# Attention's loads issued by GpSimd, with bias rows for both heads of a pair in one load

## The chip, the core and the metric

The kernel runs on one core of one Trainium2 chip. A core has five instruction queues that each run their own instructions in program order and wait for each other through semaphores: TensorE (PE in the profile, with PEld for weight loads), VectorE (DVE), ScalarE (ACT), GpSimd (POOL) and SyncE (SP, here only an issuer of DMAs). The metric is the device time of one execution in microseconds, as the median over runs.

## The reference, cut to what matters

The program is one layer of a trunk with two groups of heads, in float32, on 1024 latent tokens (a grid of 16 rows and 64 columns) and 256 context tokens. What matters for the change is neighbourhood attention: each latent query sees 8 rows by 16 columns of its grid with a learned relative bias, and all 256 cached context keys, in one softmax.

```python
def _neighbourhood_attention(q, k, v, k_ctx, v_ctx, rpb):
    ...
    bias = rpb[:, dr[:, None, :, None], dc[None, :, None, :]].astype(jnp.float32)
    s_loc = jnp.einsum('bhrqd,bhrikd->bhrqik', qg, k_band).astype(jnp.float32) * scale
    s_loc = jnp.where(col_in[None, None, None, :, None, :], s_loc + bias[None], NEG)
    s_loc = s_loc.reshape(B, H, R, W, wr * W)
    s_ctx = jnp.einsum('bhrqd,bhkd->bhrqk', qg, k_ctx).astype(jnp.float32) * scale
    p = jax.nn.softmax(jnp.concatenate([s_loc, s_ctx], axis=-1), axis=-1).astype(v.dtype)
    ...
```

Beside it stands the Hyena group, a long convolution done by Fourier transforms; then follow the output projection and the feed-forward part:

```python
    a = attend(q, k, v).transpose(0, 2, 1, 3).reshape(B, L, ATTN_WIDTH)
    hyo = _hyena(hy, k_f, filt_bias)
    merged = jnp.concatenate([_rmsnorm(a, grp_norm_g[:ATTN_WIDTH]),
                              _rmsnorm(hyo, grp_norm_g[ATTN_WIDTH:])], axis=-1)
    x = x + g1 * (merged @ w_out)
```

## The kernel before

The kernel runs through stages: modulation and filter spectra, the input projection (24 chunks of 128 columns, each split into a high and a low part and multiplied in three passes by `mm3`, L115 to L118), the hyena chains, attention, output projection, and the feed-forward part. A tile framework orders the instructions of all stages with an estimate of its own and places them in each engine's queue; within a queue nothing overtakes.

The input projection writes q, k and v to DRAM (`qd`, `kd`, `vd`). Its last two chunks are `qkv(3, 2)`, the values of the last pair of heads, and `hy_chunk(2, 3)`; `cached(3)` then turns the last cached keys and stores them with `kt` (L735).

**The hyena chains** (`chain(j)`, j = 0 to 3 for four channel blocks of the latent tokens, 4 for the context) run with a high priority beside the projection and attention. A chain does for each of two orders o: forward products (L802), their twiddles (ACT L814 and L815 feed DVE L816), butterflies on DVE (L822 to L827), the product with a filter spectrum K for each half h (L836 loads K by SP, L840 to L843 multiply), butterflies back (L847 to L852), twiddles (L857 to L859), inverse products (L871), and gates (L876 to L878 for o = 0, L882 to L884 for o = 1). SP stores the result to `hyd` (L889, L892). K has one buffer for even and one for odd chains, so half 1's K can only be loaded once L841 of half 0 has read the buffer. The output projection's weights (L1148) take the chains' memory, and so come after the last store.

**Attention** (`attend(p_)`, four pairs of heads) loads q, k, v and the cached values of its pair by SP (L1003 to L1009), and then the bias tables `tb`. There are three tables for each head of the pair (first block of columns, inner ones, last block), each of 128 query rows by 736 numbers. `bias_load` fills one table with 16 loads of 16 partitions by 4 columns by 64 numbers from `rpw` in DRAM (L958). That makes 6 x 16 = 96 loads for a pair and 384 in all, each of 64 runs of 256 bytes, and SP issues them in the same queue as the chains' K and data. A pair then goes through four blocks of 16 columns: scores (L1020) in two halves, bias added and maximum taken on DVE (L1041), exponentials on ACT (L1054, L1055), turning by PE (`turn`, L1064), eviction from PSUM by `evict`, alternately on DVE (L968) and ACT (L970), the product with v (`av_mm`, L978), and the division by the sums (`recips`, L986 to L995; L1110). `context()` does the context tokens' attention (L1082 to L1091). The tiles `sel` and `jrev`, cut from the identity, serve the division and the later row scales.

Of the kernel before, what the change touches and what calls it, by code (L numbers as in the profile page):

```python
# [11 lines left out]
F32 = mybir.dt.float32  # L12
# [7 lines left out]
P = 128  # L20
# [3 lines left out]
LT = LL + LC  # L24
NH, DH = 8, 64
# [4 lines left out]
NEG = -1e30  # L30
# [44 lines left out]
HALF_ROWS = ((0, 11), (4, 12))  # L75
# [11 lines left out]
def _build(nc, tc, top, V, A, G, T, Q, I, O, dbg, upto):  # L87
# [37 lines left out]
    ident = cst.tile([P, P], F32, name="ident")  # L125
# [373 lines left out]
    qd = dr.tile([4, P, LT], F32, name="qd")  # L499
    with ies:  # L500
# [3 lines left out]
        for gi, (s, col, tl) in enumerate(groups):  # L504
            xs = []
            for i in tl:
                src, row, _ = tiles[i]
                x = wp.tile([P, D], F32, tag="wada", name="x", bufs=4) if gi in XW else \
# [21 lines left out]
            n = P * len(tl)  # L530
# [46 lines left out]
    kd = dr.tile([4, P, LT + 256], F32, name="kd")  # L577
# [345 lines left out]
    tp = pool(es, "att", reuse_waits="tile")  # L923
    asq = tp.tile([P, LT], F32, name="asq")


    sel = tp.tile([P, 4, P], F32, name="sel")
    for h in range(2):
        for i in range(4):
            V.tensor_copy(sel[:, i, h * DH:(h + 1) * DH], ident[:, 4 * h + i:4 * h + i + 1].to_broadcast([P, DH]))  # L930
    jrev = tp.tile([P, P], F32, name="jrev")
    V.tensor_copy(jrev, ident[:, ::-1])
    lrow = [tp.tile([P, P], F32, name=f"lrow{i}") for i in range(2)]
    for t in lrow:
        V.memset(t, 0.0)
# [8 lines left out]
    for r in Pring:  # L944
        for t in r:
            G.memset(t[:, 0, :, 11:16], 0.0)
            G.memset(t[:, 1, :, 0:4], 0.0)
    def bias_load(h, var):

        t = tbs[h % 2][var]  # L950
        for half in range(2):
            for rq in range(8):
                r = 8 * half + rq
                r0 = min(max(r - 4, 0), 8)
                nr = HALF_ROWS[half][1]
                a, d = r0 - HALF_ROWS[half][0], r0 - r + 7
                tv = t[rq * 16:(rq + 1) * 16, HOFF[half]:HOFF[half] + nr * 32].rearrange("q (u x) -> q u x", u=4)
                Q.dma_start(out=tv[:, :, a * 8:a * 8 + 64], in_=rpw[var, :, h, :, d * 8:d * 8 + 64])  # L958

    def stat(name, n=2):  # L960
        return tp.tile([P, n], F32, tag=name, name=name, bufs=4)
# [1 line left out]
    def evict(ps):  # L963

        t = tp.tile([P, 512], F32, tag="pt", name="pt", bufs=4)
        evict.i += 1
        if evict.i % 2:
            V.tensor_copy(t, ps)  # L968
        else:
            A.copy(t, ps)  # L970
        return t
# [27 lines left out]

    def attend(p_):  # L1000

        q = tp.tile([P, LT], F32, tag="q", name="q", bufs=2)
        Q.dma_start(out=q, in_=qd[p_])  # L1003
        k = tp.tile([P, LT + 256], F32, tag="k", name="k", bufs=2)
        Q.dma_start(out=k, in_=kd[p_])
        vs = tp.tile([P, 12, P], F32, tag="vs", name="vs", bufs=2)
        Q.dma_start(out=vs[:, 0:10], in_=vd[:, :, p_ * P:(p_ + 1) * P].rearrange("n p x -> p n x"))
        for h in range(2):
            Q.dma_start(out=vs[:, 10:12, h * DH:(h + 1) * DH],  # L1009
                        in_=I["cache_ctx_v"][0, 0, 2 * p_ + h].rearrange("(n p) d -> p n d", p=P))  # L1010
        for var in range(3):
            for h in range(2):
# [10 lines left out]
        def scores(cb, l, l2, j):  # L1023

            u0, u1 = BLK[cb]
            nu = u1 - u0
            a0 = 2 * cb - 1 + u0
            var = (0, 1, 1, 2)[cb]
            qc = [slice((2 * cb + half) * P, (2 * cb + half + 1) * P) for half in range(2)]
            m = [stat(f"m{h}") for h in range(2)]  # L1030
            loc = [[], []]
            for half in range(2):
                r0, nr = HALF_ROWS[half]
                n = nu * nr * 8
                sl = bk("S").rearrange("p (h x) -> p h x", h=2)
                smm([sl[:, h, :n] for h in range(2)], qc[half], lambda r: kg[r, a0:a0 + nu, r0 * 8:(r0 + nr) * 8])
                for h in range(2):
                    reg = Pring[h][cb][:, half, :, r0:r0 + nr].rearrange("p u r c -> p u (r c)")
                    loc[h].append(reg)
                    tv = tbs[h][var][:, HOFF[half]:HOFF[half] + nr * 32].rearrange("p (u x) -> p u x", u=4)  # L1040
                    V.tensor_tensor_reduce(out=reg, in0=sl[:, h, :n].rearrange("p (u x) -> p u x", u=nu),  # L1041
                                           in1=tv[:, u0:u1], op0=ALU.add, op1=ALU.max, scale=1.0, scalar=-3.0e38,
                                           accum_out=m[h][:, half:half + 1])
            sc = bk("S").rearrange("p (h x) -> p h x", h=2)
            for half in range(2):
                smm([sc[:, h, half * 256:(half + 1) * 256] for h in range(2)], qc[half], lambda r: k[r, LT:])
            m2 = stat("n", 4)
            V.tensor_reduce(m2, sc.rearrange("p h (a x) -> p (h a) x", a=2), axis=AX.X, op=ALU.max, negate=True)
            pc = tp.tile([P, 2, 2, 256], F32, tag="pc", name="pc", bufs=3)
            for h in range(2):  # L1050
                V.scalar_tensor_tensor(m[h], m[h], -1.0, m2[:, 2 * h:2 * h + 2], op0=ALU.mult, op1=ALU.min)
                for half in range(2):
                    c = 4 * h + 2 * j + half
                    A.activation(loc[h][half], loc[h][half], AF.Exp, bias=m[h][:, half:half + 1], accum_out=l[:, c:c + 1])  # L1054
                    A.activation(pc[:, h, half], sc[:, h, half * 256:(half + 1) * 256], AF.Exp,  # L1055
                                 bias=m[h][:, half:half + 1], accum_out=l2[:, c:c + 1])
            Pc[cb] = pc
# [38 lines left out]
        for b in range(2):  # L1096
# [12 lines left out]
            bs = recips(l, 8)  # L1109
            V.tensor_mul(dst[:, 2 * b:2 * b + 2], av.rearrange("p (b r c) -> p b r c", b=2, r=16),  # L1110
                         bs.rearrange("p (b r c) -> p b r c", b=2, r=16))
        if p_ < 3:
            context()
            sq = asq if p_ == 0 else tp.tile([P, LT], F32, tag="q", name="sq", bufs=2)
            A.activation(sq, at4[:, p_], AF.Square)
            if p_:
                V.tensor_add(asq, asq, sq)
# [41 lines left out]

    def token_scales():  # L1160

        sq = tp.tile([P, LT], F32, tag="q", name="sq", bufs=2)
# [601 lines left out]
```

## Time and profile before

| | us |
|---|---|
| median of three runs | 1954.95 |
| the runs | 1950.76, 1954.95, 1959.55 |
| the profiled execution | 1947.16 |
| its span, first to last instruction | 1945.3 |
| mean granted TensorE clock | 0.954 |

Over the whole span PE is busy for 1739.3 us (89%), PEld for 1458.2 (75%), DVE for 1372.1 (71%), ACT for 885.5 (46%) and POOL for 256.7 (13%). The span in 40 slices of 48.6 us, with a digit for the busy tenths of each, shows where PE is not full:

```profile
PE   6899989999993686687599699999999999999998
DVE  4667648746776775776455788898877777566787
POOL 2354556531320000000010000000000000000001
```

Slices 13 to 20 (counted from 1), from about 583 to 970 us, are attention and the rest of the hyena chains. POOL does nothing there. A row of a timeline gives start, duration, engine, line, what is written from what, and in brackets how long the engine had been idle and what ended it. SPq is SP's issuing of a DMA, not the transfer.

### The profile page before, as it was taken

The numbers are of one execution on the slowest core, as the hardware profiler recorded it, in microseconds if no ns is written. First come the engines' busy times: TensorE is split into PE (matmuls) and PEld (weight loads), VectorE is DVE, ScalarE is ACT, GpSimd is POOL, SyncE is SP. The second block draws the span as 40 slices with busy tenths as digits, with TensorE's granted clock in tenths as the row PEclk, the third lists the DMA queues.
The fourth block names the chain that finished last, engine by engine and source line by source line (L and its number), as shares of the span: only waits on it lengthen the run. The fifth ranks groups of instructions, "written<-read, shape, count | busy, mean of one in ns | idle before, by whom it ended". The sixth has DMA issues, their size and how long they took to land.

```text
span 1945.3 us, 27592 instructions
## 1 busy us (share of the span) xinstructions
PE 1739.3 (89%) x9999; PEld 1458.2 (75%) x9999; DVE 1372.1 (71%) x2183; ACT 885.5 (46%) x1827; POOL 256.7 (13%) x227
## 2 busy tenths in 40 slices
PE   6899989999993686687599699999999999999998
PEld 1688877888771354354478599999999999888786
DVE  4667648746776775776455788898877777566787
ACT  4655445434332463453265544444444444443352
POOL 2354556531320000000010000000000000000001
PEclk9999989999996898898799899999999999999999
DMA  7424444455344434301433155544322222753563
GB/s 260 133 75 126 129 126 121 138 189 174 122 128 128 106 65 116 76 12 54 162 127 113 44 161 171 170 157 165 127 71 71 71 70 63 264 202 113 190 210 134
DMA packets 238266, 249.79 MB, mean 128 GB/s; under 512 B 56610, under 2 KB 187795, under 8 KB 237873
## 3 DMA queue, kind: packets, MB, share of 16 engines
q1 hardware_dynamic: 236168, 247.09, 40.5%
q8 instruction: 79, 1.29, 0.3%
q10 hardware_dynamic: 1705, 0.82, 0.2%
q14 instruction: 58, 0.48, 0.1%
q0 software_dynamic: 256, 0.11, 0.0%
HBM read 176.75 MB, written 71.20 MB: 127 GB/s over the span
## 4 chain that ended last, share of the span: by engine, by line
PE 55%; DVE 15%; DMA 11%; ACT 5%; SPq 5%; issue 5%; POOL 3%; DVEq 0%; POOLq 0%; ACTq 0%
PE psd L118 6%; PE psd L116 6%; PE psd L117 6%; SPq L958 4%; PE psp L118 4%; PE psp L116 4%; PE psp L117 4%; PE psa L116 2%; PE psa L117 2%; PE psa L118 2%; DMA wt<-in_w_down_dram 2%; PE psav L978 2%; PE psc L116 2%; PE psc L117 2%; PE psc L118 2%
## 5 line engine op out<-in xcount | busy, mean ns | idle before, releaser
L116 PE MATMUL psp<-hh,wh 128*128 128x512 f32 (+1 forms) x552 | 201.0, 364 | 2.3 <-ACT wh L121 1.9
L118 PE MATMUL psp<-hh,wl 128*128 128x512 f32 (+1 forms) x552 | 198.9, 361 | 0.5 <-POOL wl L122 0.5
L117 PE MATMUL psp<-hl,wh 128*128 128x512 f32 (+1 forms) x552 | 198.2, 359 | 0.0
L117 PE MATMUL psa<-T,ws 128*128 128x256 f32 (+1 forms) x528 | 165.2, 313 | 2.8 <-DVE T L1206 2.8
L116 PE MATMUL psa<-T,ws 128*128 128x256 f32 (+1 forms) x528 | 165.6, 314 | 2.4 <-ACT rows L1479 2.4
L118 PE MATMUL psa<-T,ws 128*128 128x256 f32 (+1 forms) x528 | 164.6, 312 | 0.0
L116 PE MATMUL psd<-wd,gs 128*128 128x512 f32 x360 | 140.3, 391 | 3.1 <-ACT gs L121 3.1
L117 PE MATMUL psd<-wd,gs 128*128 128x512 f32 x360 | 140.7, 391 | 0.0
L118 PE MATMUL psd<-wd,gs 128*128 128x512 f32 x360 | 123.9, 392 | 1.6 <-DVE gs L122 1.6
L116 PEld LDWEIGHTS psp<-hh,wh 128*128 128x128 f32 x552 | 104.8, 190 | 23.1 <-issue 6.2
L118 PEld LDWEIGHTS psp<-hh,wl 128*128 128x128 f32 x552 | 104.9, 190 | 15.2 <-issue 0.8
L116 PE MATMUL psc<-T,ws 128*128 128x384 f32 (+1 forms) x352 | 110.0, 313 | 6.8 <-ACT ws L121 6.8
L117 PEld LDWEIGHTS psp<-hl,wh 128*128 128x128 f32 x552 | 104.9, 190 | 14.0 <-issue 0.4
L1679 POOL TENSOR_TENSOR rs<-rs,mhalf 128x1 f32<-128x1 f32 x10 | 7.7, 772 | 810.7 <-DVE rs L1678 810.7
L117 PE MATMUL psb<-T,ws 128*128 128x384 f32 (+1 forms) x352 | 110.3, 313 | 0.7 <-DVE T L1206 0.7
L118 PE MATMUL psb<-T,ws 128*128 128x384 f32 (+1 forms) x352 | 110.1, 313 | 0.0
L117 PE MATMUL psc<-T,ws 128*128 128x384 f32 (+1 forms) x352 | 110.1, 313 | 0.0
L116 PE MATMUL psb<-T,ws 128*128 128x384 f32 (+1 forms) x352 | 109.8, 312 | 0.3 <-ACT T L1205 0.3
L118 PE MATMUL psc<-T,ws 128*128 128x384 f32 (+1 forms) x352 | 109.8, 312 | 0.0
L116 PEld LDWEIGHTS psa<-T,ws 128*128 128x128 f32 x528 | 101.0, 191 | 3.5 <-ACT rows L1479 3.4
L117 PEld LDWEIGHTS psa<-T,ws 128*128 128x128 f32 x528 | 101.2, 192 | 3.1 <-DVE T L1206 3.1
L118 PEld LDWEIGHTS psa<-T,ws 128*128 128x128 f32 x528 | 100.8, 191 | 0.0
(389 smaller groups left out, 4646.9 us busy)
## 6 DMA issues: line engine op xcount, KB each, us to landing
wada<-in_w_ada_dram SPq DMA_DIRECT2D x48, 512.0 KB
wr<-in_w_up_dram SPq DMA_DIRECT2D x44, 512.0 KB
gr<-gdr SPq DMA_DIRECT2D x44, 320.0 KB
wr<-in_w_in_dram SPq DMA_DIRECT2D x23, 512.0 KB
wt<-in_w_down_dram SPq DMA_DIRECT2D x44, 256.0 KB
tdr<-wt SPq DMA_DIRECT2D x44, 256.0 KB
gdr<-cv SPq DMA_DIRECT2D x22, 512.0 KB
wr<-tdr SPq DMA_DIRECT2D x20, 512.0 KB
```

Of the source, the lines that this page charges most:

```text
L116: T.matmul(out, ah, bh, start=start, stop=False, skip_group_check=True)
L117: T.matmul(out, ah, bl, start=False, stop=False, skip_group_check=True)
L118: T.matmul(out, al, bh, start=False, stop=stop, skip_group_check=True)
L958: Q.dma_start(out=tv[:, :, a * 8:a * 8 + 64], in_=rpw[var, :, h, :, d * 8:d * 8 + 64])
L978: T.matmul(av[h * DH:(h + 1) * DH, c0:c0 + 256], vt[:, h * DH:(h + 1) * DH], p[:, h * 256:(h + 1) * 256], start=start, stop=False, tile_po ...
L1679: G.tensor_tensor(rs, rs, mhalf, op=ALU.pow)
```

## The change

All of attention's loads move from SP to GpSimd. The bias tables of the two heads of a pair become one tile of 1472 columns, so `bias_load` fills both heads with one load of 16 partitions by 8 by 64 numbers: 48 loads for a pair, 192 in all, of 128 runs each. With q, k, v and the cached values POOL issues 212 DMAs for attention. q and k of the first pair and the three tables are asked for ahead of the rest of the stage (`qkload(0)`, `bias_load(0, var)`), into buffers that are placed, by tiles named "none" that only hold room, where the last but one projection chunk worked. The buffers of q and k are named by the pair's parity instead of taken in turn. `evict` gives every third eviction to DVE, not every second. The copies that make `sel` and `jrev` go from DVE to ACT.

```diff
-    HOFF = (0, HALF_ROWS[0][1] * 32)
+    HOFF = (0, HALF_ROWS[0][1] * 64)
...
-    tbs = [[tp.tile([P, NROW * 32], F32, name=f"tb{h}{v}") for v in range(3)] for h in range(2)]
-    for t in tbs:
-        for v in t:
-            G.memset(v, NEG)
...
+    tbs = [None] + [tp.tile([P, NROW * 64], F32, name=f"tb{v}") for v in (1, 2)]
+    tp.tile([P, 2, 2, 256], F32, tag="pc", name="none", bufs=3)
...
+    for tag, n in (("q0", LT), ("k0", LT + 256), ("k1", LT + 256)):
+        tp.tile([P, n], F32, tag=tag, name="none", bufs=1)
+    tp.tile([P, 12, P], F32, tag="vs", name="none", bufs=2)
+    tbs[0] = tp.tile([P, NROW * 64], F32, name="tb0")
...
-                tv = t[rq * 16:(rq + 1) * 16, HOFF[half]:HOFF[half] + nr * 32].rearrange("q (u x) -> q u x", u=4)
-                Q.dma_start(out=tv[:, :, a * 8:a * 8 + 64], in_=rpw[var, :, h, :, d * 8:d * 8 + 64])
+                tv = tbs[var][rq * 16:(rq + 1) * 16, HOFF[half]:HOFF[half] + nr * 64].rearrange("q (u x) -> q u x", u=8)
+                G.dma_start(out=tv[:, :, a * 8:a * 8 + 64],
+                            in_=rpw[var, :, 2 * p_:2 * p_ + 2, :, d * 8:d * 8 + 64].rearrange("q h u x -> q (h u) x"))
+
+    def qkload(p_):
+        q = tp.tile([P, LT], F32, tag=f"q{p_ % 2}", name="q", bufs=1)
+        G.dma_start(out=q, in_=qd[p_])
+        k = tp.tile([P, LT + 256], F32, tag=f"k{p_ % 2}", name="k", bufs=1)
+        G.dma_start(out=k, in_=kd[p_])
+        return q, k
+
+    first = qkload(0)
+    for var in range(3):
+        G.memset(tbs[var], NEG)
+        bias_load(0, var)
...
+            A.copy(sel[:, i, h * DH:(h + 1) * DH], ident[:, 4 * h + i:4 * h + i + 1].to_broadcast([P, DH]))
...
-        if evict.i % 2:
+        if evict.i % 3 == 0:
             V.tensor_copy(t, ps)
...
-        q = tp.tile([P, LT], F32, tag="q", name="q", bufs=2)
-        Q.dma_start(out=q, in_=qd[p_])
-        k = tp.tile([P, LT + 256], F32, tag="k", name="k", bufs=2)
-        Q.dma_start(out=k, in_=kd[p_])
+        q, k = qkload(p_) if p_ else first
...
-        for var in range(3):
-            for h in range(2):
-                bias_load(2 * p_ + h, var)
+        if p_:
+            for var in range(3):
+                bias_load(p_, var)
```

The framework orders the instructions of the stage anew. Three places of the new order follow; a name's number is a buffer's, `s_` tiles are a chain's, and "x8" counts equal instructions in a row.

On PE, at the start of attention, the difference of the two orders is this:

```order
 L871 MATMUL pscA<-s_5679,idft 128x256 x8
 L802 MATMUL pscA<-s_5800,dftf 128x256 x2
-L1020 MATMUL psS<-k,q 128x264 x2
-L1020 MATMUL psS<-k,q 128x288 x2
+L1038 MATMUL psS<-k,q 128x264 x2
+L1038 MATMUL psS<-k,q 128x288 x2
 L802 MATMUL pscA<-s_5800,dftf 128x256 x2
```

Only the line numbers of the scores differ: chain 1's inverse products (L871) and chain 2's first forward ones (L802) stand ahead of the first scores in both. On SP, a little later, the loads of chain 2's K stood among bias loads (L958) and now stand alone:

```order
-L1007 DMA vs<-vd 128x10x128
-L1009 DMA vs<-in_cache_ctx_v_dram 128x2x64 x2
-L958 DMA tb_6407<-rpw 16x4x64 x16
-L958 DMA tb_6410<-rpw 16x4x64 x16
-L836 DMA K<-Kd 128x1024
-L958 DMA tb_6408<-rpw 16x4x64 x11
-L836 DMA K<-Kd 128x1024
-L958 DMA tb_6408<-rpw 16x4x64 x5
-L958 DMA tb_6411<-rpw 16x4x64
+L836 DMA K<-Kd 128x1024 x2
 L788 DMA s_5894<-lxd 128x1024
```

So nothing but the chains' own loads and stores is left in SP's queue there. On DVE, at the end of attention, the last product of attention (L1110) had only chain 4 behind it:

```order
L882 TENSOR_TENSOR s_6241<-tt,pscA 128x256
L883 TENSOR_TENSOR s_6241<-tt,pscA 128x256
L884 TENSOR_TENSOR s_6241<-s_6241,s_6239 128x2x256
L1110 TENSOR_TENSOR at_6387<-psav,bs 128x2x16x16
L840 TENSOR_TENSOR s_6286<-s_6266,K 128x1024
L841 TENSOR_TENSOR s_6283<-s_6266,K 128x1024
```

Now it is L1128, and the second half of chain 3 follows it as well:

```order
L840 TENSOR_TENSOR s_6196<-s_6187,K 128x1024
L841 TENSOR_TENSOR s_6147<-s_6187,K 128x1024
L1128 TENSOR_TENSOR at_6387<-psav,bs 128x2x16x16
L842 TENSOR_TENSOR s_6147<-s_6147,s_6196 128x512
L843 TENSOR_TENSOR s_6147<-s_6147,s_6196 128x512
L840 TENSOR_TENSOR s_6203<-s_6187,K 128x1024
L841 TENSOR_TENSOR s_6147<-s_6187,K 128x1024
L842 TENSOR_TENSOR s_6147<-s_6147,s_6203 128x512
```

Here s_6147 belongs to chain 3's second order and s_6283 to chain 4. On POOL, the first pair's q, k and first table come first, then its values, then the second pair's q, k and values, and only then the first pair's other two tables; that second q waits, among others, for the store of `kt` (L735) by `cached(3)`. 21 of the 212 loads stand ahead of it.

More of the change, by code (lines that the diff above doesn't have):

```diff
@@ L924, in _build, with bias_load @@
     asq = tp.tile([P, LT], F32, name="asq")
-    sel = tp.tile([P, 4, P], F32, name="sel")
-    for h in range(2):
[L929 to L935, printed above, removed]
-    tbs = [[tp.tile([P, NROW * 32], F32, name=f"tb{h}{v}") for v in range(3)] for h in range(2)]
-    for t in tbs:
-        for v in t:
-            G.memset(v, NEG)
     BLK = ((1, 4), (0, 4), (0, 4), (0, 3))
     Pring = [[tp.tile([P, 2, b - a, 16, 8], F32, name=f"Pl{h}{i}") for i, (a, b) in enumerate(BLK)] for h in range(2)]
[L944 to L950, printed above, removed]
+    tbs = [None] + [tp.tile([P, NROW * 64], F32, name=f"tb{v}") for v in (1, 2)]
+    tp.tile([P, 2, 2, 256], F32, tag="pc", name="none", bufs=3)
+    tp.tile([P, 512], F32, tag="pt", name="none", bufs=4)
+    tp.tile([P, LT], F32, tag="q1", name="none", bufs=1)
+    for name, n in (("l", 8), ("l2", 8), ("m0", 2), ("m1", 2), ("n", 4), ("lc", 4)):
+        tp.tile([P, n], F32, tag=name, name="none", bufs=4)
+    tp.tile([P, 512], F32, tag="bs", name="none", bufs=2)
+    for tag, n in (("q0", LT), ("k0", LT + 256), ("k1", LT + 256)):
+        tp.tile([P, n], F32, tag=tag, name="none", bufs=1)
+    tp.tile([P, 12, P], F32, tag="vs", name="none", bufs=2)
+    tbs[0] = tp.tile([P, NROW * 64], F32, name="tb0")
+    def bias_load(p_, var):
         for half in range(2):
@@ L956, in bias_load @@
                 a, d = r0 - HALF_ROWS[half][0], r0 - r + 7
-                tv = t[rq * 16:(rq + 1) * 16, HOFF[half]:HOFF[half] + nr * 32].rearrange("q (u x) -> q u x", u=4)
-                Q.dma_start(out=tv[:, :, a * 8:a * 8 + 64], in_=rpw[var, :, h, :, d * 8:d * 8 + 64])
+                tv = tbs[var][rq * 16:(rq + 1) * 16, HOFF[half]:HOFF[half] + nr * 64].rearrange("q (u x) -> q u x", u=8)
[11 more added lines that the diff above has]
+        bias_load(0, var)
+        if var == 0:
+            for r in Pring:
+                for t in r:
+                    G.memset(t[:, 0, :, 11:16], 0.0)
+                    G.memset(t[:, 1, :, 0:4], 0.0)
+    sel = tp.tile([P, 4, P], F32, name="sel")
+    for h in range(2):
+        for i in range(4):
+            A.copy(sel[:, i, h * DH:(h + 1) * DH], ident[:, 4 * h + i:4 * h + i + 1].to_broadcast([P, DH]))
+    jrev = tp.tile([P, P], F32, name="jrev")
+    A.copy(jrev, ident[:, ::-1])
+    lrow = [tp.tile([P, P], F32, name=f"lrow{i}") for i in range(2)]
+    for t in lrow:
+        V.memset(t, 0.0)
     def stat(name, n=2):
@@ L1000, in attend @@
     def attend(p_):
[L1002 to L1005 removed]
+        q, k = qkload(p_) if p_ else first
         vs = tp.tile([P, 12, P], F32, tag="vs", name="vs", bufs=2)
[L1007 removed]
+        G.dma_start(out=vs[:, 0:10], in_=vd[:, :, p_ * P:(p_ + 1) * P].rearrange("n p x -> p n x"))
         for h in range(2):
[L1009 removed]
+            G.dma_start(out=vs[:, 10:12, h * DH:(h + 1) * DH],
                         in_=I["cache_ctx_v"][0, 0, 2 * p_ + h].rearrange("(n p) d -> p n d", p=P))
[L1011 to L1013 removed]
+        if p_:
+            for var in range(3):
+                bias_load(p_, var)
         kg = k[:, 0:LL].rearrange("p (u x) -> p u x", u=8)
```

6 lines of the change are left out of this document (3 added, 3 removed).

## Prediction

> **What bounds the kernel now.** I read the busy time of each engine in stretches first, to see where the code that changes runs. The columns are the stretch, its length, then busy time (and instructions) of PE, PEld, DVE, ACT and POOL, the granted clock, the DMA share and GB/s.
>
> ```profile
> 577.00:624.00 47.00, 12.76 (x44) 8.79 (x44) 29.98 (x55) 10.11 (x30) 0.00 (x0) 0.67 0.42 113
> 624.00:904.00 280.00, 213.20 (x1284) 125.22 (x1284) 195.52 (x426) 143.91 (x472) 0.00 (x0) 0.91 0.29 73
> 904.00:949.00 45.00, 19.57 (x63) 12.00 (x61) 21.79 (x31) 6.38 (x11) 0.00 (x0) 0.83 0.23 77
> ```
>
> Attention's matmuls run from 624 to 904 us, and PE is idle in 67 of these 280 us. Ahead of it lie 47 us with PE nearly empty, behind it 45 us in which only the last hyena chain runs. No engine is full, so the waits decide. PE's and DVE's timelines (start, duration, what, and in brackets the idle time before and what ended it) have these large ones:
>
> ```profile
> 613.94 1.19 PE L871 MATMUL pscA<-s,idft 128*128 128x256 f32 x2 [29.11 <-DVE s L859]
> 624.12 1.20 PE L1020 MATMUL psS<-k,q 64*128 64x264 f32 x8
> 671.09 1.12 PE L978 MATMUL psav<-pt,vs 128*64 128x256 f32 x4 [12.24 <-DVE pt L968]
> 745.01 1.12 PE L978 MATMUL psav<-pt,vs 128*64 128x256 f32 x4 [9.24 <-DVE pt L968]
> 818.31 1.12 PE L978 MATMUL psav<-pt,vs 128*64 128x256 f32 x4 [9.20 <-DVE at L1110]
> ...
> 604.78 1.23 DVE L840 TENSOR_TENSOR s<-s,K 128x1024 f32<-128x1024 f32 x1 [7.08 <-DMA K<-Kd]
> 624.99 0.43 DVE L1041 CUSTOM_DVE_ANT_0 Pl<-psS,tb 128x264 f32<-128x264 f32 x1 [1.32 <-DMA tb<-rpw]
> 666.80 1.23 DVE L840 TENSOR_TENSOR s<-s,K 128x1024 f32<-128x1024 f32 x1 [10.65 <-DMA K<-Kd]
> 741.99 1.23 DVE L840 TENSOR_TENSOR s<-s,K 128x1024 f32<-128x1024 f32 x1 [9.21 <-DMA K<-Kd]
> 815.29 1.23 DVE L840 TENSOR_TENSOR s<-s,K 128x1024 f32<-128x1024 f32 x1 [9.03 <-DMA K<-Kd]
> ```
>
> Read the two lists together. Each of PE's three long waits for an eviction or a product of DVE ends just after DVE's wait for a filter spectrum K (L840), which stands ahead of that eviction in DVE's order. So K is what is late. SP's rows, and the source line of the bias loads (count, shortest, median and longest duration in ns), say why:
>
> ```profile
> L958 SPq DMA_DIRECT2D tb<-rpw x384: 302/424/1779, 587.3 to 822.9; - x192
> ...
> 651.24 1.22 DVE L841 TENSOR_TENSOR s<-s,K 128x1024 f32<-128x1024 f32 x1
> 645.83 17.05 SPq L958 DMA_DIRECT2D tb<-rpw  x32
> 662.97 0.37 SPq L836 DMA_DIRECT2D K<-Kd  x1
> ...
> 662.97 3.80 DMA K<-Kd
> 930.69 3.63 DMA K<-Kc
> ```
>
> K has one buffer per chain parity. It was free when L841 ended at 652.5, but SP stood in a run of 32 bias loads, one per 0.53 us, and issued K only at 662.97. The transfer then took 3.80 us, little more than the 3.63 us late in the stage with no bias load about. The bound of the stage is thus SP's issuing order, through K, DVE and PE.
>
> **The change, part by part.**
>
> *Loads leave SP.* All 384 bias loads go, and 192 of twice the rows are issued by POOL. At 666.80 K could have been asked for at 652.5 and have landed at 656.3; DVE reached its turn at 656.1 (666.80 less 10.65), so the wait shrinks to about 0.2 us. The other two are alike, and in the new order eight to ten instructions of DVE (L842 and L843 among them) stand between the two L840 of such a pair, in which K can land. I book PE's waits, 12.24 + 9.24 + 9.20 = **30.7 us**; bounds 20 (a third falls back to other waits) and 33 (PE also loses its low-clock start, some 0.7 us each time).
>
> *The first pair's early loads.* q, k and the first bias table can be in SBUF before 600 us instead of 624. But PE's order has the same eight inverse products of a chain (L871) and two forward ones ahead of the first scores as before, and PE's 29.11 us wait is for DVE in that chain, not for attention's loads. So only the table's own lateness goes, the 1.32 us at 624.99, and the share of SP in the K wait at 604.78:
>
> ```profile
> 595.16 1.22 DVE L841 TENSOR_TENSOR s<-s,K 128x1024 f32<-128x1024 f32 x1
> ...
> 622.97 0.69 DVE L884 TENSOR_TENSOR s<-s,s 128x512 f32<-128x512 f32 x1
> ```
>
> L841 ended at 596.4; K from SP then lands at 600.2 in place of 604.78. That is 4.3 us, with the table 5.6; bounds 4 and 6. The early loads alone are worth little.
>
> *The end of attention.* In the new DVE order chain 3 is further behind when attention ends: its last product (L1128) stands right behind the first L841 of the chain's second half, while before only chain 4 was left. What follows is priced from rows of the same work standing alone:
>
> ```profile
> 623.09 1.10 PE L802 MATMUL pscA<-s,dftf 128*128 128x256 f32 x4 [1.43 <-DVE s L883]
> ...
> 903.38 1.11 PE L802 MATMUL pscA<-s,dftf 128*128 128x256 f32 x4
> 903.39 0.69 DVE L1110 TENSOR_TENSOR at<-psav,bs 128x512 f32<-128x512 f32 x1 [1.20 <-ACT bs L995]
> 907.48 1.22 DVE L840 TENSOR_TENSOR s<-s,K 128x1024 f32<-128x1024 f32 x1 [3.40 <-ACT s L805]
> ...
> 945.79 2.78 DMA hyd<-s
> ```
>
> From the end of L841: 3.8 us for K; 18.3 us from L840 to the next chain's first forward product (604.78 to 623.09); 4.1 us from that product to chain 4's L840 (903.38 to 907.48); 38.3 us to its store (907.48 to 945.79). Together 64.5 us, where before 42.4 us lie between L1110's start and the store. That is **22.1 us lost**; bounds 16 and 26. The output projection's weights wait for this store, so it is on the path in full.
>
> *What leaves attention in exchange.* That half of chain 3 no longer takes turns with the last blocks:
>
> ```profile
> 872.54 1.91 PE L978 MATMUL psav<-pt,vs 128*64 128x256 f32 x8 [1.66 <-DVE pt L968]
> 884.70 0.65 PE L1064 MATMUL psX<-ident,Pl 128*128 128x128 f32 x4 [2.71 <-DVE pt L968]
> 889.44 0.74 PE L871 MATMUL pscA<-s,idft 128*128 128x256 f32 x2
> 893.53 1.46 PE L871 MATMUL pscA<-s,idft 128*128 128x256 f32 x6
> 898.33 1.89 PE L871 MATMUL pscA<-s,idft 128*128 128x256 f32 x8
> ```
>
> 1.66 + 2.71 us of waits behind its DVE work and 4.1 us of its products: **8.5 us gained**; bounds 0 (other waits take their place) and 12.
>
> *Evictions and setup.* A third instead of half of the 96 evictions goes to DVE. The columns of the groups are busy us, mean ns, idle before.
>
> ```profile
> L968 DVE COPY pt<-psX 128x512 f32<-128x512 f32 x48 | 32.9, 685 | 12.0 <-PE psX L1064 12.0
> L842 DVE TENSOR_TENSOR s<-s,s 128x512 f32<-128x512 f32 x14 | 9.6, 684 | 0.2
> L1054 ACT ACTIVATE Pl<-Pl,m 128x264 f32<-128x264 f32 (+1 forms) x64 | 35.7, 558 | 26.5 <-DVE m L1051 26.3
> L1055 ACT ACTIVATE pc<-psS,m 128x256 f32<-128x256 f32 x64 | 29.7, 466 | 0.0
> L970 ACT COPY pt<-psX 128x512 f32<-128x512 f32 x48 | 28.2, 588 | 62.8 <-PE psX L1064 62.7
> ```
>
> Sixteen move: 11.0 us off DVE, 9.4 us onto ACT, whose evictions waited 62.7 us for PE and so have room. I take zero; bounds -9.4 and +11. The copies that make sel go to ACT in the same stretch and cancel alike.
>
> *POOL as issuer.* POOL is idle here (0.00 above). Its DMAs at the kernel's start and the transfer that holds up its queue:
>
> ```profile
> 2.04 0.58 POOL L295 DMA_DIRECT2D w<-in_filt_w_dram  x1
> 4.97 0.56 POOL L309 DMA_DIRECT2D GE<-in_t_z_dram  x1
> ...
> 582.71 1.72 DMA kd<-kt
> ...
> 872.92 0.45 DVE L1041 CUSTOM_DVE_ANT_0 Pl<-psS,tb 128x288 f32<-128x288 f32 x1
> ```
>
> A load of 64 rows held POOL 0.58 us, one of 17 rows 0.56. A bias load has 128 runs, which the trace does not show: bounds 0.56 and 1.16 (twice 64 rows). I take 0.6, as row count hardly told. The second pair's q waits until kd<-kt has landed at 584.4, and 191 of POOL's 212 loads stand from there on. The last table is wanted 31 us before attention's end (872.9 against 904.1), which I expect at 858.6 (945.8 - 22.7 - 64.5). With 2 us to land, loads cost nothing up to (858.6 - 31 - 586.4) / 191 = 1.26 us each. Both bounds lie below, so the term is zero.
>
> **Sum.** 30.7 + 5.6 - 22.1 + 8.5 = 22.7 us gained. The profiled execution took 1947.16 us (span 1945.3), so it would take 1924.5. It lies 7.8 us below the median of the three runs, 1954.95; on that median the forecast is **1932 us**. All bounds together give -11 and +46.
>
> **The rivals.**
>
> *POOL becomes the bound (slower).* Place: the last pair's tables, behind all other loads. From 1.38 us a load the gain is gone, from 1.43 the kernel is slower by over 0.5%. That takes descriptors which POOL cannot write while DVE works: 0.56 us plus a whole L841 of 1.22 is 1.78. At 1.6, the store comes at 586.4 + 306 + 31 + 64.5 = 988, 42 later: 1997 us. Against: both rows of POOL's DMAs show under 0.6 us. For: the 192 loads stand beside dense DVE work, and those rows, at the kernel's start, do not. The Trainium skill (SBUF — State Buffer, Who interferes with whom) has GpSimd's descriptor writing shut out only while DVE is in a two-port mode, as in copies within SBUF, and not by a tensor_tensor. Here the evictions read PSUM at 685 ns, as slow as L842's 684 for the same size, so by that rule the price stays at zero. Chance 0.09.
>
> *K is late for the transfers' sake, not SP's.* If the bias rows crowd the DMA engines, the 30.7 and 4.3 us stay and the sum is -12: 1967 us. The rows above speak against it: 3.80 beside 3.63 us. The Trainium skill (DMA: Bandwidth & Descriptors, Issuing engines are not separate DMA queues) says this: DMAs share 16 engines whoever starts them, and another issuer saves only sequencer time, usually small beside the transfer. The trace disagrees on small: 10.5 us of issuing against 3.80. Chance 0.04.
>
> *Evictions late on ACT (no change).* A score block puts eight exponentials on ACT, 4 x (0.558 + 0.466) = 4.1 us. If in each of 16 blocks one more eviction waits a quarter of that behind them, 16 us go, and 6 remain: 1949. For: two evictions in a row are now ACT's. Against: its 62.7 us of waiting. Chance 0.16.
>
> *The early loads let scores start early.* If PE fell to scores at 588, some 32 us more: 1900. PE's order speaks against it. Chance 0.07.
>
> **How the numbers follow.** The forecast has 0.64. Faster by over 0.5% (9.8 us, about what a measurement can tell from no change): 0.64 + 0.07 = 0.71; within it 0.16; slower 0.09 + 0.04 = 0.13. The range, 1909 to 1960, is the sum with its bounds (46 gained, 5 lost), takes in the no-change rival, and leaves out the two slower rivals and the early start: 0.20.
>
> **What would show it.** L840's waits for K between 640 and 820 gone, with K issued within 1 us of the L841 that frees it; first scores near 620, not near 590; the end of attention near 859 and the store about 64 us behind it; POOL's bias loads near 0.6 us each. Wrong would be: K waits of 9 us again, POOL without a pause to the last table, or a store as far behind attention's end as before.

## The result, and the profile after

The changed kernel took 1921.29 us (median of four runs, 1920.5 to 1925.38) beside 1954.28 us (1950.76 to 1959.55) for the kernel before: ratio 0.9833, with a 95% interval of 0.9806 to 0.986. That is 27 to 38 us faster. The forecast was 1932. The profiled execution took 1925.38 us, and the working gave 1924.5 from the profiled execution before; the two profiled executions lie on different sides of their medians, 7.1 us below the one and 4.1 above the other.

The stretches of the span of the changed kernel (columns as in the prediction) are cut at the first scores, the end of the last division by sums, and the last store of `hyd`; the first row is the kernel before between its first scores and its last division.

```profile
624.12:904.09 279.97, 213.17 (x1284) 125.30 (x1284) 195.60 (x426) 143.91 (x472) 0.00 (x0) 0.91 0.29 73
```

```profile
623.42:847.91 224.49, 197.87 (x1265) 116.63 (x1264) 169.97 (x387) 146.41 (x474) 82.22 (x154) 0.99 0.28 72
847.91:920.21 72.30, 37.65 (x80) 22.46 (x80) 36.85 (x52) 11.49 (x25) 0.00 (x0) 0.57 0.19 58
```

Attention is 55.5 us shorter, and PE's idle time in it fell from 66.8 to 26.6 us. But what follows attention grew from 42.4 to 73.0 us, counted from the start of the last division, and PE's clock there is 0.57. The waits that the prediction spoke of stand in DVE's and SP's timelines now as follows.

```profile
604.15 1.23 DVE L840 TENSOR_TENSOR s<-s,K 128x1024 f32<-128x1024 f32 x1 [3.35 <-DMA K<-Kd]
652.45 1.22 DVE L840 TENSOR_TENSOR s<-s,K 128x1024 f32<-128x1024 f32 x1
720.05 1.23 DVE L840 TENSOR_TENSOR s<-s,K 128x1024 f32<-128x1024 f32 x1 [1.08 <-DMA K<-Kd]
787.14 1.22 DVE L840 TENSOR_TENSOR s<-s,K 128x1024 f32<-128x1024 f32 x1
847.21 0.68 DVE L1128 TENSOR_TENSOR at<-psav,bs 128x512 f32<-128x512 f32 x1
851.17 1.23 DVE L840 TENSOR_TENSOR s<-s,K 128x1024 f32<-128x1024 f32 x1 [2.08 <-DMA K<-Kd]
...
920.21 0.37 SPq L892 DMA_DIRECT2D hyd<-s  x1
```

```profile
623.42 1.20 PE L1038 MATMUL psS<-k,q 64*128 64x264 f32 x8
860.23 1.22 PE L871 MATMUL pscA<-s,idft 128*128 128x256 f32 x2 [12.51 <-DVE s L859]
```

The three waits of 9 to 11 us for K are gone, and first scores come 0.7 us earlier. From the first scores to the last store, PE's only wait above 3 us now lies behind attention, for chain 3. POOL's bias loads, by their source line (count, shortest, median and longest duration in ns), took 531 ns each and hardly scattered:

```profile
L951 POOL DMA_DIRECT2D tb<-rpw x192: 528/531/573, 572.3 to 778.7; - x192
```

### The profile page after: what moved, and what is told of

It is laid out like the page before. It is cut to its first block, busy times and chain, and to the rows that moved or that the text cites. A ratio compares the mean times of both kernels' runs of the same rounds, so it can differ in the third digit from the quotient of the medians.

```text
span 1923.4 us, 27377 instructions
## 1 busy us (share of the span) xinstructions
PE 1742.3 (91%) x9999; PEld 1460.2 (76%) x9999; DVE 1358.3 (71%) x2158; ACT 893.5 (46%) x1852; POOL 371.1 (19%) x436
## 4 chain that ended last, share of the span: by engine, by line
PE 35%; DVE 14%; DMA 8%; issue 4%; ACT 4%; POOL 2%; SPq 0%; DVEq 0%; POOLq 0%; ACTq 0%
PE psd L118 5%; PE psd L116 5%; PE psd L117 5%; DMA wt<-in_w_down_dram 2%; PE psa L116 2%; PE psa L117 2%; PE psa L118 2%; DMA tdr<-wt 2%; POOL tb L951 2%; PE psc L117 1%; PE psc L118 1%; PE psc L116 1%; PE pscA L871 1%; PE psb L117 1%; PE psb L118 1%
## 5 line engine op out<-in xcount | busy, mean ns | idle before, releaser
L951 POOL DMA_DIRECT2D tb<-rpw x192 | 100.4, 531 | 35.7 <-DVE m L1059 20.3
L871 PE MATMUL pscA<-s,idft 128*128 128x256 f32 x160 | 55.1, 487 | 56.0 <-DVE s L859 45.1
L116 PEld LDWEIGHTS psa<-T,ws 128*128 128x128 f32 x528 | 101.4, 192 | 4.7 <-ACT rows L1497 4.7
```

The lines of the kernel that those rows point to most:

```text
L116: T.matmul(out, ah, bh, start=start, stop=False, skip_group_check=True)
L871: T.matmul(pa[:, i * 256:(i + 1) * 256], idft[:, i, h], Ys[:, h, i, xs], start=h == 0, stop=h == 1, skip_group_check=True)
L951: G.dma_start(out=tv[:, :, a * 8:a * 8 + 64], in_=rpw[var, :, 2 * p_:2 * p_ + 2, :, d * 8:d * 8 + 64].rearrange("q h u x -> q (h u) x"))
```

## The experiments

All numbers of the traces are in one table: "first scores" is the start of the first matmul of the scores, "attention" the time from there to the start of the last division, "tail" from that to the last store of `hyd`, and "both done" the time at which attention and the chains are finished. In two kernels the chains finish first.

| kernel | ratio to before, interval | first scores | attention | tail | both done |
|---|---|---|---|---|---|
| before | 1 | 624.1 | 279.3 | 42.4 | 945.8 |
| changed | 0.9833 [0.9806, 0.986] | 623.4 | 223.8 | 73.0 | 920.2 |
| after_again (the same) | 0.985 [0.9822, 0.9878] | 622.1 | 222.5 | 72.2 | 916.8 |
| sp_loads | 0.9858 [0.9823, 0.9892] | 624.6 | 225.3 | 67.2 | 917.1 |
| merge_only | 0.9843 [0.9812, 0.9874] | 623.2 | 249.8 | 45.7 | 918.7 |
| k_by_pool | 1.0006 [0.9991, 1.0022] | 620.3 | 261.8 | 69.6 | 951.6 |
| half_evict | 0.9894 [0.9857, 0.993] | 618.8 | 234.1 | 65.7 | 918.6 |
| late_loads | 0.9921 [0.9895, 0.9948] | 626.7 | 231.1 | 70.4 | 928.2 |
| split_loads | 1.0229 [1.0202, 1.0256] | 623.8 | 368.9 | - | 992.7 |
| warm_tail | 0.9873 [0.9844, 0.9901] | 621.7 | 222.8 | 72.1 | 916.6 |
| context_first | 0.9877 [0.9846, 0.9908] | 621.4 | 236.8 | 59.5 | 917.6 |
| context_hole | 0.9806 [0.9778, 0.9833] | 657.8 | 222.1 | 26.8 | 906.7 |
| merge_hole | 0.9824 [0.9804, 0.9845] | 659.3 | 245.1 | 3.7 | 908.1 |
| two_in_hole | 0.9974 [0.9958, 0.999] | 734.5 | 215.0 | - | 949.5 |

The yardstick, the changed kernel once more beside three of the others:

> The changed kernel itself, beside the next three on one chip, as their yardstick: ratio 0.981 to 0.986; attention 224 us long, hyd's last store 73 us behind its last division.

It came out as expected, and shows how far one profile can be trusted: both done 3.4 us earlier than in the first profile, and 3.8 us less behind that, where the instructions are the same.

### Who issues, or how many: sp_loads and merge_only

sp_loads lets SP issue all of attention's loads in the changed kernel; of the five lines that this changes, the one of the bias loads is shown:

```diff
-                G.dma_start(out=tv[:, :, a * 8:a * 8 + 64],
+                Q.dma_start(out=tv[:, :, a * 8:a * 8 + 64],
```

> The changed kernel with attention's loads issued by SP again, still 192 merged bias loads. If K is late because it stands behind bias loads in SP's queue (theory), DVE waits for K again between 600 and 850 us, by at least 5 us in two or three places (SP needs about 0.45 us for each of some 8 to 16 loads ahead of a K), attention lasts 235 to 260 us from its first scores to its last division (224 in the changed kernel, 279 in the kernel before), and the time lies 0.5 to 1.5% above the changed kernel's (ratio 0.988 to 1.000). If halving the count of loads was what helped, the waits stay below 2 us each and the ratio is that of the changed kernel, 0.983.

The stated theory held at the first of its places and fell at the others. DVE's wait for K near 600 us is back, ahead of the first scores:

```profile
603.91 1.23 DVE L840 TENSOR_TENSOR s<-s,K 128x1024 f32<-128x1024 f32 x1 [6.67 <-DMA K<-Kd]
```

But the waits that follow, between 640 and 850 us, are 1.31 us at most with all 192 loads in SP's own queue, attention lasts 225.3 us, and the ratio is within the intervals of the changed kernel. So the sharper cut: merge_only is the kernel before with merged loads and nothing else. It keeps the old order on PE, ACT and DVE, but for one reciprocal that comes two instructions later on DVE.

```diff
-    tbs = [[tp.tile([P, NROW * 32], F32, name=f"tb{h}{v}") for v in range(3)] for h in range(2)]
+    tbs = [tp.tile([P, NROW * 64], F32, name=f"tb{v}") for v in range(3)]
...
-                Q.dma_start(out=tv[:, :, a * 8:a * 8 + 64], in_=rpw[var, :, h, :, d * 8:d * 8 + 64])
+                Q.dma_start(out=tv[:, :, a * 8:a * 8 + 64],
+                            in_=rpw[var, :, 2 * p_:2 * p_ + 2, :, d * 8:d * 8 + 64].rearrange("q h u x -> q (h u) x"))
...
-            for h in range(2):
-                bias_load(2 * p_ + h, var)
+            bias_load(p_, var)
```

> The kernel before with one edit: the bias rows of both heads come in one load, 192 loads on SP in place of 384. PE, ACT and DVE keep the order of the kernel before instruction for instruction. Theory (what counts is the number of loads that stand in the queue, since SP takes about 0.43 us to issue one, of 64 runs or of 128): the waits for K between 600 and 820 us fall to 2 us or less each, attention shrinks from 279 us to 236 to 250 (30.7 us of PE's waits, and up to 8 us of its higher clock), the tail stays at 42 us, and the ratio is 0.978 to 0.986. Rival (the loads have to leave SP): two or more waits for K of 5 us or more stay, attention lasts over 262 us and the ratio is above 0.990.

In merge_only's trace: the stretch of attention; SP's bias loads by their source line; SP's and DVE's rows at the first K wait and at the place where the kernel before lost most.

```profile
623.15:873.68 250.53, 211.27 (x1284) 124.72 (x1284) 195.22 (x426) 144.19 (x472) 0.00 (x0) 0.95 0.27 70
```

```profile
L957 SPq DMA_DIRECT2D tb<-rpw x192: 302/429/2060, 584.5 to 775.6; - x192
```

```profile
584.52 14.32 SPq L957 DMA_DIRECT2D tb<-rpw  x24
598.95 0.37 SPq L836 DMA_DIRECT2D K<-Kd  x1
...
638.66 12.40 SPq L957 DMA_DIRECT2D tb<-rpw  x20
651.51 0.34 SPq L836 DMA_DIRECT2D K<-Kd  x1
```

```profile
591.76 1.22 DVE L841 TENSOR_TENSOR s<-s,K 128x1024 f32<-128x1024 f32 x1
602.68 1.23 DVE L840 TENSOR_TENSOR s<-s,K 128x1024 f32<-128x1024 f32 x1 [8.38 <-DMA K<-Kd]
...
650.27 1.21 DVE L841 TENSOR_TENSOR s<-s,K 128x1024 f32<-128x1024 f32 x1
655.78 1.23 DVE L840 TENSOR_TENSOR s<-s,K 128x1024 f32<-128x1024 f32 x1 [0.61 <-DMA K<-Kd]
```

A load of 128 runs costs SP 429 ns in the median, one of 64 runs cost 424 (the row of L958 in the prediction). Half as many loads are about half the time in SP's queue: at the second place K is asked for at 651.51, right behind L841, where before it was 10.5 us late. At the first place it isn't enough: L841 ends at 592.98, but 24 loads keep SP until 598.8, and DVE waits 8.38 us, against 7.08 in the kernel before. The expectation had 2 us or less there too. With the order unchanged, attention shrinks by 29.4 us, 27.5 of them idle time of PE and 1.9 its shorter matmuls at the higher clock. The ratio, 0.9843, is the changed kernel's. **The merge of the two heads' loads brings all of the gain that the ratios can tell; what the move to POOL, the early loads and the evictions add in sum is less than the intervals, some 6 us to each side.** By the traces they do gain some 5 us ahead of the first scores, as is told below under the early loads.

k_by_pool asks the question from the other side: all 384 loads stay on SP, and only K leaves it.

```diff
-                Q.dma_start(out=Kt.rearrange(f1), in_=(Kd[o, j] if lat else Kc[o])[:, h * 1024:(h + 1) * 1024])
+                (G if 2 * j + o > 2 else Q).dma_start(out=Kt.rearrange(f1), in_=(Kd[o, j] if lat else Kc[o])[:, h * 1024:(h + 1) * 1024])
```

> The kernel before with nothing changed but the issuer of K from chain 1's second order on: POOL in place of SP; all 384 bias loads stay on SP. Theory (queue order): the waits of 7 to 11 us for K vanish, attention from its first scores to its last division shrinks from 279 us by 25 to 50 us, although the same bytes move. What stands behind the last division grows to about 46 chain instructions on DVE (28 before), so the store of hyd follows it by 65 to 72 us; in sum a ratio of 0.985 to 0.998. Rival (the transfers crowd each other): waits for K of 5 us or more stay, attention shrinks by less than 10 us, and with the longer tail the kernel is slower than before by 0.5 to 1%.

K's long waits go here too, so the transfers were not what made K late, though the same bytes move. But SP, with 384 loads, is now late with something else; PE's two worst waits in attention and DVE's longest for a table:

```profile
676.93 1.65 PE L1020 MATMUL psS<-k,q 64*128 64x384 f32 x4 [6.22 <-DVE m L1041]
754.64 2.21 PE L1020 MATMUL psS<-k,q 64*128 64x264 f32 x8 [13.98 <-DMA q<-qd]
```

```profile
676.25 0.52 DVE L1041 CUSTOM_DVE_ANT_0 Pl<-psS,tb 128x352 f32<-128x352 f32 x1 [6.40 <-DMA tb<-rpw]
```

Attention is 17.5 us shorter, not the 25 to 50 that were expected, since these two waits cost PE 20.2 us; with the longer tail that the new order has, the time is that of the kernel before. A queue with 384 loads is late for whoever stands in it.

### The other parts: half_evict, late_loads

```diff
-        if evict.i % 3 == 0:
+        if evict.i % 2:
```

> The changed kernel with evictions again half on DVE and half on ACT. As the prediction had it, the ratio matters little: within 5 us of the changed kernel (ratio 0.981 to 0.986), apart from the order behind attention, where 46 chain instructions on DVE are left for 52. If a part of the 25 us that attention gained beyond the three K waits came from taking evictions off DVE, attention lasts 8 to 15 us longer than the changed kernel's 224 us and the ratio is 0.987 to 0.991.

Attention lasts 10.3 us longer than in the changed kernel, 6.1 of them idle time of PE (32.7 against 26.6), but six chain instructions fewer stand behind it, and the tail is 7.3 us shorter. From first scores to "both done" it is 299.8 us, against 296.8 and 294.7 in the two profiles of the changed kernel. So by the traces the new division of the evictions is worth 3 to 5 us, part of which may be the order's. The ratio, 0.9894, lies where the second expectation had it, 0.4 to 0.6% above the changed kernel's two (some 9 to 12 us), with intervals that touch or overlap; the size stays open between these.

late_loads takes the early loads back:

```diff
-    first = qkload(0)
...
-        bias_load(0, var)
...
-        q, k = qkload(p_) if p_ else first
+        q, k = qkload(p_)
...
-        if p_:
-            for var in range(3):
-                bias_load(p_, var)
+        for var in range(3):
+            bias_load(p_, var)
```

> The changed kernel with the first pair's q, k and tables asked for only where attention begins, like those of the other pairs. Theory: PE comes to the first scores only behind chain 1, near 623 us, and POOL can issue q, k, v and the first table (21 loads of 0.53 us and some for v) in 14 us after 585, so nothing is lost: within 3 us of the changed kernel (ratio 0.982 to 0.985), and the first K wait near 600 us is shorter than the 3.35 us of the changed kernel, since the turned keys' loads are not delayed. Rival: the early loads are what lets attention start, and first scores come at 628 us or later with the ratio 0.986 or more.

The theory was wrong about the cost: the median is 10 to 14 us above the changed kernel's two (on other chips), and both done is 8 to 11 us later. At the entry the trace shows why. POOL, which has nothing else to wait for, sends q, k and v just when `cached(3)` loads the last keys, and these are late. Rows of POOL, SP and PE:

```profile
574.83 0.63 POOL L956 DMA_DIRECT2D q<-qd  x1
575.46 0.56 POOL L958 DMA_DIRECT2D k<-kd  x1
576.01 0.99 POOL L1023 DMA_DIRECT2D vs<-vd  x1
```

```profile
578.48 1.14 SPq L728 DMA_DIRECT2D ck<-in_cache_ctx_k_dram  x2
```

```profile
586.52 0.66 PE L732 MATMUL pstB<-ident,ck 128*128 128x128 f32 x2 [7.18 <-DMA ck<-in_cache_ctx_k_dram]
```

In the kernel before PE waited 1.64 us at this place. SP's order had put q behind the last keys' store there, so merge_only needs no early loads; they mend what the move to POOL upsets. Without them first scores come 3.3 to 4.6 us later. The rest of the loss, an attention that is 7 to 9 us longer, came with a new order and isn't traced to one wait.

### Is POOL the bound, or the order: split_loads

```diff
-                G.dma_start(out=tv[:, :, a * 8:a * 8 + 64],
-                            in_=rpw[var, :, 2 * p_:2 * p_ + 2, :, d * 8:d * 8 + 64].rearrange("q h u x -> q (h u) x"))
+                for h in range(2):
+                    G.dma_start(out=tv[:, 4 * h:4 * h + 4, a * 8:a * 8 + 64],
+                                in_=rpw[var, :, 2 * p_ + h, :, d * 8:d * 8 + 64])
```

> The changed kernel with every bias load halved again: 384 loads on POOL, one per head. In its order no chain instruction is left behind attention's last division on DVE. Theory: a load costs POOL about 0.5 us whatever its runs, so POOL issues for some 204 us of 260, without being what attention waits for; attention takes in the rest of the chains and lasts 245 to 275 us, the store of hyd comes within 10 us of its end, and the time is 0.960 to 0.980 of the kernel before. Rival (POOL becomes the bound, as in the prediction's rival): tables come late, PE waits for tb or DVE's maxima for 10 us or more in every pair, attention lasts over 290 us and the time is above that of the changed kernel.

The time is what the rival said, and its reason is not. The source line of the bias sums, with what DVE waited for ahead of them:

```profile
L1060 DVE CUSTOM_DVE_ANT_0 Pl<-psS,tb x64: 421/486/558, 624.7 to 977.8; 128x264 f32<-128x264 f32 x16, 128x288 f32<-128x288 f32 x16, 128x352 f32<-128x352 f32 x16, 128x384 f32<-128x384 f32 x16
...
its engine sat idle before it (us, times) until:
  PE psS L1039: 3.8, 5
```

DVE never waited for a table, so POOL's 384 loads, 512 ns each, were in time. What is new is the order, which puts chain work ahead of the scores. That the framework's estimate takes so many loads for slow would explain it, but is inferred. One such place, in a window and on PE:

```profile
640.00:662.00 22.00, 3.76 (x24) 1.99 (x20) 18.44 (x26) 2.45 (x6) 20.07 (x41) 0.61 0.37 102
```

```profile
660.39 2.08 PE L1039 MATMUL psS<-k,q 64*128 64x256 f32 x8 [18.15 <-DVE m L1060]
```

DVE is busy for 18.4 of these 22 us, nearly all with a chain, while PE waits for two maxima that stand behind it. The chains are done at 897 us, and attention goes on alone until 992.7.

One more row bears on the rival that K comes late for the transfers' sake. No load of attention stands in SP's queue here, and K is asked for at 596.44, right behind L841, but DVE gets it only at 603.57, and the row of the transfer says why:

```profile
596.44 7.10 DMA K<-Kd
```

POOL had asked for q, k and v of the second pair from 591.56 on, 2 MB together, and the DMA engines are busy for 0.77 of these 7 us. That those loads are what slowed K is argued from the times alone.

### What follows attention: warm_tail, context_first, context_hole, merge_hole, two_in_hole

The tail was longer than forecast, at a low clock. warm_tail fills PE's idle time in the context chain:

```diff
                 pa = bk("cA")
+                if not lat and rp == 0:
+                    for _ in range(8):
+                        T.matmul(pa, dftf[:, 0, 0:P], dftf.rearrange(f1), start=True, stop=True, skip_group_check=True)
```

> The changed kernel with eight matmuls of 512 columns on constants ahead of the context chain's inverse products, into the bank that those overwrite; they only fill PE's idle time while DVE works. If the tail is longer than forecast because PE's granted clock is low there (0.57, and four forward products take 2.07 us where they took 1.13 in the kernel before), the clock behind attention rises to 0.65 or more, the way from the context chain's first product with K to the store shrinks from 42.5 to 37 to 40 us, and the time falls by 3 to 6 us. If the clock is not what lengthens it, the way stays at 42 to 44 us or grows by the extra matmuls.

Rows of PE in the changed kernel (after_again) and in warm_tail, forward products of the context chain's first order and, in warm_tail, the extra matmuls of its second:

```profile
872.98 2.07 PE L802 MATMUL pscA<-s,dftf 128*128 128x256 f32 x4 [0.68 <-ACT s L805]
```

```profile
872.34 1.13 PE L802 MATMUL pscA<-s,dftf 128*128 128x256 f32 x4 [0.68 <-ACT s L805]
...
899.69 9.93 PE L870 MATMUL pscA<-dftf 128*128 128x512 f32 x16 [0.68 <-ACT s L805]
```

The clock rose to 0.78, and the way from the first product with K to that of the second order shrank from 24.48 to 21.85 us. Then it fell again: the extra matmuls, slow themselves, kept PE until the real ones were late, and the second order took 22.47 us in place of 19.33. The whole way, 44.3 us against 43.8, did not shrink to the 37 to 40 that were expected, and the median, taken side by side, is 5.4 us longer. So the low clock costs some 2.6 us in one order of this chain; that it can be had back was not shown.

context_first has the context chain ahead of chain 2:

```diff
-    def chain(j):
+    def chain(j, b_):
...
-        b_ = j % 2
...
-    for j in range(5):
-        if j == 2:
+    for i, j in enumerate((0, 1, 4, 2, 3)):
+        if i == 2:
...
-            chain(j)
+            chain(j, i % 2)
```

> The changed kernel with the chains in the order 0, 1, 4, 2, 3, so that the context chain works where the first scores begin, and not at the end. Theory: what follows attention is on the path in full; only chain 3's second order is left there, 35 to 50 us in place of 73, and attention grows by 5 to 20 us for the context chain's work: the time falls by 10 to 30 us against the changed kernel (ratio 0.967 to 0.979). Rival: the first scores wait for the chain that is put ahead, and attention starts later by as much as the end gains: within 5 us of the changed kernel.

The rival came true in the time, though not by its reason: scores did not come later. Attention grew by 13 to 14 us and the tail lost as much. The context chain's products have only the chains' one PSUM bank there, behind chain 1, and the chain ran within attention. context_hole lets it go earlier, by three banks until it is done (the cut is against context_first):

```diff
-        if i == 2:
+        if i == 3:
```

> The changed kernel with the chains in the order 0, 1, 4, 2, 3 as before in context_first, and the chains' three PSUM banks kept until the context chain is done (one bank from the third chain on before). Then the context chain's products need not wait for the bank of chain 1's inverse products, and it works in the stretch before the first scores where PE is nearly empty and DVE has 17 of 47 us free. Theory: first scores come later by 10 to 18 us (the context chain's 22 us of DVE work less what fits into free time), attention lasts as in the changed kernel (220 to 232 us), and only half an order of chain 3 is left behind it, 25 to 32 us in place of 72: the time falls by 25 to 35 us against the changed kernel, ratio 0.966 to 0.973. Rival: as in context_first, chain work costs its full time wherever it stands, and the ratio stays within 0.5% of the changed kernel's 0.985.

Now the context chain does run before the scores. The tail is 26.8 us, as expected, and both done is 906.7. But the scores come at 657.8, some 35 us later than in the changed kernel, where 10 to 18 were expected, and so the 25 to 35 us of the theory did not come: the ratio, 0.9806, lies within the rival's 0.5% of 0.985. On one chip context_hole took 1911.33 us (1909.66 to 1914.53) and merge_only 1918.64 (1917.98 to 1919.85). **It has the lowest ratio here and is faster than merge_only, side by side.** Ahead of the changed kernel it is by some 6 us in the medians, which were not taken side by side; the intervals overlap, so that stays open. PE at the new place, where the chain waits for itself while the scores stand behind it:

```profile
630.75 5.43 PE L870 MATMUL pscA<-s,idft 128*128 128x256 f32 x12 [5.16 <-DVE s L841]
```

The last two ask whether the rest of the change helps there, and whether more fits in:

> merge_only with the chains in the order 0, 1, 4, 2, 3 and the three banks kept for the context chain, as in context_hole, but with loads on SP, evictions half and half and no early loads. In its order three chain instructions are left on DVE behind attention's last division. Theory: where chain work stands between the first scores and the last store hardly matters, since attention grows by what the tail loses; only the merged loads and the stretch before the scores count. Then the store of hyd comes 3 to 10 us behind attention's end, attention lasts 240 to 260 us from scores near 657 us, and the time is that of context_hole within 0.4% (ratio 0.977 to 0.985). Rival: POOL as issuer, early loads and fewer evictions on DVE are worth 10 us or more in sum, and this one stays above 0.986.

merge_hole is merge_only with the edits of context_hole. It has 0.9824 where context_hole has 0.9806, with no load on POOL, none early, and evictions half and half: as the theory had it, and with overlapping intervals.

> The changed kernel with the chains in the order 0, 1, 2, 4, 3 and three banks kept until the context chain is done: chain 2's first half and the context chain both stand ahead of the first scores, and no chain instruction is left behind attention on DVE. If PE's and DVE's free time before the scores is what can still be filled, the time falls below context_hole's (ratio 0.970 to 0.980), with first scores at 675 to 695 us. If the two chains only queue for DVE there, scores come after 695 us and the ratio is 0.981 to 0.995.

two_in_hole has the order 0, 1, 2, 4, 3, and closes the three banks at i == 4. Scores came at 734.5 us, after 695 as the rival had it, and the ratio, 0.9974, is above the rival's too: the chains work alone ahead of them, and PE is busy for 54.3 of the 152.5 us from 582 on. Two of its waits there, both for DVE:

```profile
647.64 1.19 PE L870 MATMUL pscA<-s,idft 128*128 128x256 f32 x2 [24.89 <-DVE s L858]
685.73 1.19 PE L870 MATMUL pscA<-s,idft 128*128 128x256 f32 x2 [24.37 <-DVE s L858]
```

## Why the prediction was right, point by point

The time fell into the range, and the sign was right. Between the two profiled executions the sum was nearly exact, 22.7 us forecast and 21.8 measured, but that is luck in part. Between the medians it is 33.0, and with after_again's profiled execution 29.0. Two terms missed their bounds, in opposite directions, and made up for each other; 3.7 us were lost behind the last store, where the instructions are the same. The range's upper end, 1960, allows for 5 us lost where the bounds add up to 11; nothing hung on it.

- **K's waits, 30.7 us.** Right in size: 29.4 us in merge_only, where nothing else moves. The cause was given too widely. "Loads leave SP" had two halves, fewer loads and another issuer, and the prediction did not part them. The first alone does it for these three waits (merge_only, sp_loads). The second alone, with 384 loads and the old order, wasn't tried; in split_loads, with 384 loads on POOL and an order of its own, the waits for K between 640 and 850 us are 2.61 us at most as well. For the wait near 600 us only the loads' leaving SP, or K's, helped: 6.67 and 8.38 us with the merged loads on SP, 3.35 in the changed kernel, 3.01 in k_by_pool, and 5.82 in split_loads, where the transfer was slow. The Trainium skill's rule that another issuer saves only sequencer time (DMA: Bandwidth & Descriptors, Issuing engines are not separate DMA queues) stands in that sense: sequencer time was what counted, but fewer starts saved it as well.
- **First pair's early loads and first K wait, 5.6 us.** First scores come 0.7 us earlier (2.0 in after_again), but the work ahead of them had moved too: PE turns the last keys (L732) at 581.83 us before, at 583.97 in the changed kernel and at 582.41 in after_again. From there to the first scores it takes 42.3 us before, and 39.5 and 39.7 in the two profiles of the changed kernel, so the term measures 2.6 to 2.8 us. With the 192 loads on SP it takes 44.7 (merge_only) and 44.5 (sp_loads). K was asked for right behind L841, as forecast, and by the numbers given that is 604.78 less 600.2, 4.6 us and not 4.3. Two things took from it: K came 4.65 us after its issue at 599.50, where 3.80 was taken, beside POOL's loads; and the first L840 stands 13.1 us behind the keys, 12.2 before, most likely since the nine copies for `sel` and `jrev`, now on ACT, stand ahead of the chain's twiddles (13.4 in sp_loads and half_evict, which have them there too, and 12.2 in merge_only and k_by_pool, which have them on DVE). The table's 1.32 us was misread: in the changed kernel DVE is idle there for the same 1.32 us, put down to PE's first scores, and in both kernels the instruction starts 0.87 us behind them. "The early loads alone are worth little" was true against the kernel before, and false within the changed one (late_loads).
- **Longer tail, -22.1 us.** The mechanism was right, the size short: -30.6 us, beyond the bound of 26. Of its four stretches the two short ones measured 4.0 and 4.3 us for 3.8 and 4.1. The half of chain 3 took 22.2 for 18.3 (20.4 in after_again), and the context chain 42.5 for 38.3 (43.8). The row of the context chain was priced with PE's clock at 0.82; now it is 0.54 there, and four forward products take 2.07 us, not the 1.13 at 907.50 in the kernel before. warm_tail ties 2.6 us of the excess to the clock. The half of chain 3 was priced at 0.58 and had 0.54, so most of its excess stays open.
- **What leaves attention, +8.5, and evictions, 0.** Together 26.0 us (merge_only's 249.8 to 223.8), beyond both upper bounds taken together, 23. half_evict puts 3 to 5 of them down to the evictions; most of the rest is chain work that moved from attention to the tail. The step that failed is pricing the two places apart: against merge_only the tail's +27.3 and attention's -26.0 cancel, where the prediction had a net loss of 13.6.
- **POOL as issuer, 0.** Right: 0.531 us a load where 0.6 was taken, no scatter beside dense DVE work (573 ns at most), and no wait of DVE for a table even with 384 loads. The rival that POOL becomes the bound is refuted for this kernel. The Trainium skill (SBUF — State Buffer, Who interferes with whom) has it that DVE's reading from PSUM and its tensor_tensor leave POOL's descriptors alone; the 192 loads of 528 to 573 ns agree.
- **The other rivals.** K late for the transfers' sake: refuted by k_by_pool as the cause of the three waits. In small it is seen: the 0.85 us just told, and the 7.10 us of one transfer in split_loads. Evictions late on ACT: the opposite is seen. Ahead of the product with v PE waits 1.5 us for DVE's evictions and 2.6 for ACT's, where half_evict has 6.5 and 0.9. Scores at 588: not seen.

## What to carry to other kernels

Count the DMA starts that stand ahead of a critical load in its queue; merging them did here most of what another queue does, without upsetting the order of anything else. Where two streams of work share engines, price the time until both are done, since what leaves the one stretch comes back in the other. And where a framework orders by its own estimates, an edit whose loads all come in time can still cost 2% through the order it brings.

## What the runs showed of the hardware

A DMA start costs its issuer nearly the same for 64 and for 128 runs of 256 bytes: 424 and 429 ns in the median on SP (before, merge_only), 512 and 531 ns on POOL (split_loads, the changed kernel). A transfer of K, 512 KB, took 3.80 and 3.63 us in the prediction's rows of the kernel before and 7.10 us in split_loads; the DMA engines were busy for 0.58 of the time in the first of these (662.97 to 666.80) and for 0.77 in the last.
